# Split values kept in DRAM, the mask built first, affine rows on GpSimd's queue, the attention's merge in halves, and raw tiles of their own for the last output weights

## The chip, the cores and the metric

The kernel runs on one core of a Trainium2 chip. A core has TensorE (PE, with its weight loads PEld), VectorE (DVE), ScalarE (ACT), GpSimd (POOL) and SyncE (SP), which run side by side and wait for each other by semaphores; transfers between DRAM and on-chip memory go through 16 DMA engines, from queues that an engine issues to. The metric is the device time of one execution in microseconds (us); a lower time is better.

## The reference

The kernel computes two layers on 1024 rows of width 1024, in float32. Each layer has a token mixer and then an MLP, each inside `x = LayerNorm(alpha * x + gate * f(x * (1 + scale) + shift))`. Layer 0's mixer is a gated MLP; layer 1's is the attention that the change is about.

```python
def mixer_b(h, w_qkv, w_out, slopes):
    qkv = (h @ w_qkv).reshape(B, S, N_PAT, 3, B_HEADS, B_HEAD_DIM)   # 3 patterns, 16 heads of 64
    for g, (window, dilation) in enumerate(((128, 1), (512, 4), (2048, 16))):
        o, lse = dilated_branch(qkv[:, :, g, 0], qkv[:, :, g, 1], qkv[:, :, g, 2], window, dilation, slopes)
        ...
    wts = softmax(stack(lses, axis=0), axis=0)[..., None]
    o = sum(wts * stack(outs, axis=0), axis=0)
    return o.reshape(B, S, 1024) @ w_out
# dilated_branch: s = q k^T / 8 - slope * dilation * diff, masked to 0 <= diff <= span, softmax, times v
def squared_relu_mlp(h, w_up, w_down):
    return square(relu(h @ w_up)) @ w_down
```

## The kernel before, in words

Every large product is made of three matmuls on float32r operands: each operand is split into a high part (a cast, mostly on ACT, line 102) and a low part (source minus high part, mostly on DVE, line 103), and high x high, high x low and low x high are added up in PSUM. `split` issues the pair. So behind every matmul operand stands one ACT and one DVE operation.

The program runs through the stages in this order: mixer of layer 0, its MLP, `values` (lines 1123 to 1249), `attention` (1252 to 1626), the output projection (`OutRows`), the second MLP. A scheduler orders each engine's instructions by the program's own order and its estimates, except where `tc.keep_in_program_order` pins one; an engine then runs its list strictly in that order. A DMA issue stands in the list of the engine that issues it; here that is always SP. Tiles come from pools in which a tag names a set of buffers; a tile whose tag has n buffers waits until the one n before it is no longer used.

`values` makes the v part of the projection for the three patterns g = 2, 1, 0. Each is a matrix product in seven block products (Strassen's scheme in Winograd's form), in the order 1, 2, 5, 6, 7, 4, 3 (`V_STEPS`), each of four groups (m = 0..3) of twelve matmuls. Product p takes a left form from the activations (`L11`, `L12`, `S1`, `S2`, `S3`, `L22`, `S4`; each in four blocks, high and low) and a right form from the weights (`vrhi`, `vrlo`). The generator `second` builds the forms S1 to S4 and L22 while the first products run; one step of it is taken per group, and a product whose form isn't built takes the steps it still needs. `evict` takes a finished group out of PSUM into `vpart` (ACT copies it, or DVE adds it to an earlier one) and stores finished blocks of v in `v_dram`.

`attention` goes over head pairs hp = 0..7 and patterns g = 2, 1, 0. Each (hp, g) has eight slots, each slot two positions, into which functions are put with `at(slot, position)`; between them the stream of q and k projections runs (`project`, line 1332, psq and psk), which TensorE fills the time with, and which is five chunks of work ahead. In a slot stand scores (`sc`), the exponentials (line 1411), transposes (`pT`), the split of the transposed probabilities (`pThi` on ACT, `pTlo` on DVE) and the product with v (`pv`, line 1459). `near` and `far` are the mask and distance tiles, built on POOL, from which POOL makes a `bias` for each head (line 1393). `qlo` holds the low part of q. `load_v` loads v for a pair, 512 KB, as `v_raw` and splits it into the tile `v`.

Two pieces of work are spread over the slots. `affine_row(i)` applies LayerNorm's gain and bias (`aff_g`, `aff_b`) on POOL to eight rows of tiles that were spilled to DRAM, at slots 2 + 2i; its loads and stores stand on SP. `merge(hp)` puts the three patterns of a pair together: it reads their maxima and sums, makes the three factors, spreads them over partitions by DMA (`bc`), multiplies each pattern's output by its `bc` (line 1543, three operations of 128x1024) and adds them up (line 1546, two operations), at slots base + 5 to base + 7, where base is 8 (3 hp + 3), that is while the next pair's first pattern runs.

At the end the output projection takes eight weight rows `wo_0` to `wo_7` in chunks of two (`unit`: load `wo_raw`, multiply by the gate on POOL, split) and the merged outputs `oraw_k`; weights and outputs from number 4 on share two `raw` buffers. `Residual` loads the rows that are added (`res`, line 289).

## Time and profile before

| | us |
|---|---|
| median of 3 runs (lowest, highest) | 2790.56 (2788.13, 2792.9) |
| the profiled execution's own time | 2792.79 |
| its span | 2791.1 |
| PE busy | 2697.5 (97%) |
| DVE busy | 2036.5 (73%) |
| ACT busy | 1424.1 (51%) |
| POOL busy | 189.2 (7%) |
| mean granted TensorE clock | 0.987 |
| moved by DMA | 416.63 MB, 149 GB/s |

A busy engine is one with an instruction in execution; an instruction that waits is not counted. A row of a timeline gives start, duration, engine, line and operation, its output and inputs by the program's names with buffer numbers left out, and in brackets the idle time of that engine just before it, with what ended it. A row with x2 stands for two instructions that overlap. The profile is of one execution, 2.2 us above the median of the runs.

### The profile page before, as it was taken

To read this page: it belongs to the slowest core of one execution; us is meant where nothing else is said; L and a number is where in the kernel's file an instruction comes from. 1 tells how busy PE (TensorE), PEld (TensorE's weight loads), DVE (VectorE), ACT (ScalarE), POOL (GpSimd) and SP (SyncE) were. 2 spreads that over 40 slices of the span, in tenths; PEclk is the share of its full clock that TensorE was granted. 3 is DMA by queue.
4 is the path that set the end of the run, shared out by engine and by line. 5 is a ranking of instruction groups with operands and counts; after the bars stand their busy time and mean duration, and the time that the engine had idled before them with its cause. 6 is when DMAs were issued, how large, how long until landed. Compare 5 with 4: busy or idle time off the path is not lost.

```text
span 2791.1 us, 36348 instructions
## 1 busy us (share of the span) xinstructions
PE 2697.5 (97%) x12954; PEld 2244.4 (80%) x12954; DVE 2036.5 (73%) x3600; ACT 1424.1 (51%) x2639; POOL 189.2 (7%) x147
## 2 busy tenths in 40 slices
PE   6999999999999999989999999999998999999998
PEld 5787878887888888878888888888876788878887
DVE  6777797777967795445767767767679975668887
ACT  3354375555443553325665666666563755554332
POOL 1001000000000000043111111111020000000000
PEclk9999999999999999999999999999999999999999
DMA  7533347667845545353222213222234564486562
GB/s 257 166 121 107 120 158 226 219 223 273 295 142 191 165 144 158 121 187 101 62 62 78 74 51 85 77 55 78 85 89 154 171 209 154 158 284 210 171 200 90
DMA packets 317690, 416.63 MB, mean 149 GB/s; under 512 B 49164, under 2 KB 174516, under 8 KB 317508
## 3 DMA queue, kind: packets, MB, share of 16 engines
q1 hardware_dynamic: 317508, 414.31, 46.4%
q8 instruction: 101, 1.65, 0.3%
q14 instruction: 81, 0.66, 0.1%
HBM read 317.69 MB, written 96.55 MB: 148 GB/s over the span
## 4 chain that ended last, share of the span: by engine, by line
PE 73%; DVE 14%; DMA 7%; ACT 3%; issue 2%; POOL 1%; SPq 1%; POOLq 0%; DVEq 0%; ACTq 0%
PE psd L949 21%; PE psua L790 8%; PE psq L1332 8%; PE psk L1332 7%; PE psv L1237 7%; PE psuc L790 4%; PE psd_wout L367 3%; DMA adaw<-in_ada_w_dram 3%; PE pv L1459 2%; PE psu L367 2%; PE psd_wo L367 2%; PE psub L790 2%; PE psv L464 1%; DMA bc<-w_dram 1%; PE sc L1404 1%
## 5 line engine op out<-in xcount | busy, mean ns | idle before, releaser
L790 PE MATMUL psua<-right,left 128*128 128x512 f32 x1536 | 366.2, 392 | 3.3 <-ACT right L102 1.7
L949 PE MATMUL psd<-rhi,lhi 128*128 128x512 f32 x896 | 350.5, 391 | 3.0 <-ACT part L821 3.0
L949 PE MATMUL psd<-rlo,lhi 128*128 128x512 f32 x896 | 350.4, 391 | 0.2
L949 PE MATMUL psd<-rhi,llo 128*128 128x512 f32 x896 | 349.8, 390 | 0.0
L790 PEld LDWEIGHTS psua<-right,left 128*128 128x128 f32 x1536 | 288.1, 189 | 65.5 <-DVE right L103 2.9
L1413 ACT ACTIVATE p<-p,stat 128x128 f32<-128x128 f32 (+1 forms) x384 | 171.2, 446 | 147.2 <-DVE stat L1411 142.4
L949 PEld LDWEIGHTS psd<-rhi,lhi 128*128 128x128 f32 x896 | 168.9, 189 | 39.6 <-ACT part L821 3.9
L949 PEld LDWEIGHTS psd<-rlo,lhi 128*128 128x128 f32 x896 | 168.9, 188 | 36.1 <-DVE rlo L103 1.1
L949 PEld LDWEIGHTS psd<-rhi,llo 128*128 128x128 f32 x896 | 169.0, 189 | 35.1
L1332 PE MATMUL psk<-form_L,wk_hi 128*128 128x512 f32 x576 | 186.9, 406 | 9.7 <-DVE qlo L103 9.7
L790 PE MATMUL psuc<-right,left 128*128 128x512 f32 x768 | 187.8, 391 | 0.0
L1332 PE MATMUL psq<-form_L,wq_hi 128*128 128x512 f32 x576 | 184.9, 402 | 0.0
L103 DVE TENSOR_TENSOR pTlo<-pT,pThi 128x512 fp32r<-128x512 f32 (+1 forms) x160 | 99.6, 623 | 108.8 <-ACT pThi L102 108.5
L128 DVE SCALAR_TENSOR_TENSOR adaacc<-adaw,silu_c,adaacc 128x512 f32<-128x512 f32 x168 | 132.4, 799 | 56.0 <-DMA adaw<-in_ada_w_dram 55.1
L790 PEld LDWEIGHTS psuc<-right,left 128*128 128x128 f32 x768 | 143.4, 188 | 30.0 <-DVE right L103 0.5
L103 DVE TENSOR_TENSOR left<-ws,left 128x512 fp32r<-128x512 f32 x128 | 87.9, 688 | 73.0 <-ACT left L102 71.3
L103 DVE TENSOR_TENSOR llo<-lraw,lhi 128x1024 fp32r<-128x1024 f32 x112 | 136.3, 1217 | 0.8 <-ACT lhi L102 0.8
L102 ACT CAST left<-ws 128x512 fp32r<-128x512 f32 x128 | 79.3, 620 | 96.2 <-DVE ws L711 85.5
L1411 DVE CUSTOM_DVE_ANT_0 p<-sc,bias 128x128 f32<-128x128 f32 (+1 forms) x384 | 122.0, 346 | 8.7 <-PE sc L1405 6.2
L102 ACT CAST rhi<-rraw 128x1024 fp32r<-128x1024 f32 x48 | 50.6, 1054 | 142.9 <-issue 113.7
L1332 PEld LDWEIGHTS psk<-form_L,wk_hi 128*128 128x128 f32 x576 | 101.0, 191 | 25.2 <-issue 10.1
L1237 PE MATMUL psv<-vrhi,form_S 128*128 128x512 f32 x384 | 119.4, 389 | 0.2 <-DVE vpart L1214 0.2
(286 smaller groups left out, 6325.8 us busy)
## 6 DMA issues: line engine op xcount, KB each, us to landing
lraw<-forms SPq DMA_DIRECT2D x112, 512.0 KB
adaw<-in_ada_w_dram SPq DMA_DIRECT2D x192, 256.0 KB
up<-in_mlp_w_up_dram SPq DMA_DIRECT2D x64, 512.0 KB
forms<-s SPq DMA_DIRECT2D x128, 256.0 KB
rraw<-in_mlp_w_down_dram SPq DMA_DIRECT2D x64, 512.0 KB
forms<-part SPq DMA_DIRECT2D x96, 256.0 KB
vraw<-in_b_w_qkv_dram SPq DMA_DIRECT2D x26, 512.0 KB
spill<-acc SPq DMA_DIRECT2D x24, 512.0 KB
```

The lines of the kernel that those rows point to most:

```text
L102: first = A.copy(hi, src) if hi_engine is A else hi_engine.tensor_copy(hi, src)
L103: return first, lo_engine.tensor_tensor(lo, src, hi, op=ALU.subtract)
L128: ins = V.scalar_tensor_tensor(acc[:], raw[:], silu_c[:, k : k + 1], acc[:], ALU.mult, ALU.add)
L367: T.matmul(dst, s[a], m[b], start=(n == 0), stop=(n == last))
L464: T.matmul(sums[u, half][:], units[u][a_][:, k * P : (k + 1) * P], hT[half][b_][:, k, :], start=k == 0 and a_ + b_ == 0, stop=k == KD - 1 ...
L790: T.matmul(acc, w[:, a, k, :], right[p][:, b, k, :], start=p in (1, 2, 5) and k + a + b == 0, stop=k == 3 and a == 1, skip_group_check=True)
L949: ins = T.matmul(sums[kind, m][:], l[a][:, k, m * P : (m + 1) * P], r[b][:, k, :], start=p in (1, 5, 2, 3) and kp + k + a + b == 0, stop=k ...
L1237: T.matmul(acc, left[:, a, 2 * kp + k, m * P : (m + 1) * P], r[b][:, k, :], start=p in (1, 2, 5) and kp + k + a + b == 0, stop=kp == 1 and ...
L1332: T.matmul(p[:], wu[a][:, k * P : (k + 1) * P], h_op(k, half, b), start=k + c_ == 0, stop=k == KD - 1 and c_ == 2)
L1411: V.tensor_tensor_reduce(out=pr[:, 0:w], in0=scb[:, sl], in1=st["bias"][:, width - w :], scale=-0.125, scalar=3e38, op0=ALU.add, op1=ALU.m ...
L1413: A.activation(pr[:, 0:w], pr[:, 0:w], AF.Exp, bias=nm, scale=-1.0, accum_out=l)
L1459: T.matmul(pvs[b][:, q0 % HALF : q0 % HALF + w_], stt, x_[:, o_ : o_ + w_], start=not begun[b], stop=left[b] == 0, skip_group_check=True)
```

## The change

Five things are done.

- `evict` no longer stores v as it is: it splits it (ACT and DVE, `vs`, two buffers) and stores both parts, 512 KB a group instead of 256; product 4 is split straight out of PSUM. `load_v` then loads the split tile directly, 1 MB, a position earlier, and has no split. `second` makes a form's `S3` block right after the `S2` block of the same number, in a step of its own, so that one `S3` temporary is enough where four were kept.
- `near`, `far` come before the `qlo` memsets, in another pool.
- The affine rows are loaded and stored by DMAs on POOL's own queue; loads at slots 2 + 3i, the two operations, pinned, at slots 3 + 3i.
- The merge's five operations become ten of half the width, pinned (but for the last pair), one to a position from slot base + 6 to base + 10; the last pair's stand from base + 10 on, two to a position.
- At the end `oraw_4` and `oraw_5` come as one 1 MB load into a v buffer, and `oraw_6`, `wo_6`, `wo_7` have tiles of their own in a pool `late`.

```diff
 def unit(src, name, gate=None, pinned=False, lo_engine=V, to=None, raw=None):
-        raw = wts.tile([P, D], F32, name=f"{name}_raw", tag="raw", bufs=2)
+        if raw is None:
+            raw = wts.tile([P, D], F32, name=f"{name}_raw", tag="raw", bufs=2)[:]
...
@@ values
-            xp = pool(ph, "x_v", 12)
+            xp = pool(ph, "x_v", 9)
+            parted = pool(ph, "parted_v", 2)
...
                 for k in range(4):
-                    s3.append(x_tile(f"s3_{k}"))
-                    sub(s3[k][:], form["L11"][:, 0, k, :], l21[k][:])
-                    plus_lo("L11", k, s3[k][:])
+                    s3 = x_tile(f"s3_{k}")
+                    sub(s3[:], form["L11"][:, 0, k, :], l21[k][:])
+                    plus_lo("L11", k, s3[:])
                     place("L22", k, x22[k][:])
-                    sub(x22[k][:], x22[k][:], s3[k][:])
+                    sub(x22[k][:], x22[k][:], s3[:])
                     place("S2", k, x22[k][:])
                     yield
+                    place("S3", k, s3[:])
+                    yield
                 built.add("S2")
-                for k in range(4):
-                    place("S3", k, s3[k][:])
-                    yield
                 built.update(("S3", "L22"))
...
             def evict(g, p, m):
                 acc = sums["pb" if p in (2, 5, 3) else "pa", m][:]
-                if p in (1, 5, 6, 4):
+                if p in (1, 5, 6):
                     t = parts[p, m] = x_tile(f"vpart_{g}_{p}_{m}")
                     A.copy(t[:], acc)
-                else:
...
+                    return
+                if p != 4:
+                    t = parts.pop(({2: 1, 7: 5, 3: 6}[p], m))
                     V.tensor_tensor(t[:], acc, t[:], op=ALU.add)
+                    acc = t[:]
+                v = parted.tile([P, 4, 4, HEAD], F32R, name=f"vs_{g}_{p}_{m}", tag="vs")
+                split(v[:, :, 0:4:3, :], v[:, :, 1:3, :], acc.rearrange("p (h e c) -> p h e c", e=2, c=HEAD))
...
+                nc.sync.dma_start(v_dram[g][i * P : (i + 1) * P, 4 * dh : 4 * dh + 4, :],
+                                  v[:].rearrange("p h f c -> p h (f c)").bitcast(F32))
@@ attention
-                @at(max(base - 4, 0), 1)
+                @at(max(base - 4, 0), 0)
                 def load_v():
...
-                    my["v"] = vs = qp.tile([P, NT, 4, HEAD], F32R, name=f"v_{hp}_{g}", tag="v")
-                    split(vs[:, :, 0:4:3, :], vs[:, :, 1:3, :], raw[:].rearrange("p t (e c) -> p t e c", e=2))
@@ merge
-                    V.tensor_tensor(bc, o, bc, op=ALU.mult)
+                    n = o.shape[1] // 2
+                    o, bc = (t[:, half * n : (half + 1) * n] for t in (o, bc))
+                    in_order(V.tensor_tensor(bc, o, bc, op=ALU.mult))
...
+                for n, f in enumerate(steps):
+                    n = n + 12 if hp < N_PAIRS - 1 else n // 2 + 10
+                    at(base + n // 2, n % 2)(f)
@@ affine rows
+                affine["row"] = row_bc(f"aff_{i}")
+                nc.gpsimd.dma_start(affine["row"][:], spill[1][i * P : (i + 1) * P, :])
+
+            def affine_row(i):
+                t = affine["row"]
+                for n, op in (("g", ALU.mult), ("b", ALU.add)):
+                    tc.keep_in_program_order(G.tensor_tensor(t[:], t[:], affine[n][:], op=op))
+                nc.gpsimd.dma_start(spill[1][i * P : (i + 1) * P, :], t[:])
 
             for i in range(NT):
-                at(2 + 2 * i, 1)(lambda i=i: affine_row(i))
+                at(2 + 3 * i, 0)(lambda i=i: affine_load(i))
+                at(3 + 3 * i, 1)(lambda i=i: affine_row(i))
@@ the output weights
+                    both = qp.tile([P, 2, S], F32, name="oraw_4", tag="v")
+                    nc.sync.dma_start(both[:], o_dram[4:6].rearrange("k p t -> p k t"))
...
+        late = pool(ph, "late", 1)
+        for n in ("w6", "w7", "o6"):
+            out.raws[n] = late.tile([P, D], F32, name=f"late_{n}")[:]
```

What this does to the order on POOL where the attention begins (a row: line, operation, output<-inputs with buffer numbers, shape); before:

```order
L1577 TENSOR_TENSOR aff_1_10499<-aff_1_10499,aff_g_10412 128x1024
L1578 TENSOR_TENSOR aff_1_10499<-aff_1_10499,aff_b_10414 128x1024
L1577 TENSOR_TENSOR aff_2_10585<-aff_2_10585,aff_g_10412 128x1024
L1578 TENSOR_TENSOR aff_2_10585<-aff_2_10585,aff_b_10414 128x1024
L1577 TENSOR_TENSOR aff_3_10663<-aff_3_10663,aff_g_10412 128x1024
L1578 TENSOR_TENSOR aff_3_10663<-aff_3_10663,aff_b_10414 128x1024
L1271 IOTA near_10127 128x256
L1272 AFFINE_SELECT near_10127<-near_10127 128x256
L1274 AFFINE_SELECT near_10127<-near_10127 128x256
```

and after:

```order
L1596 TENSOR_TENSOR aff_0_10513<-aff_0_10513,aff_g_10509 128x1024
L1596 TENSOR_TENSOR aff_0_10513<-aff_0_10513,aff_b_10511 128x1024
L1597 DMA spill_1_105<-aff_0_10513 128x1024
L1273 IOTA near_10243 128x256
L1284 MEMSET qlo0_0_10254 64x1024
L1274 AFFINE_SELECT near_10243<-near_10243 128x256
L1284 MEMSET qlo1_0_10256 64x1024
L1276 AFFINE_SELECT near_10243<-near_10243 128x256
L1591 DMA aff_1_10634<-spill_1_105 128x1024
L1596 TENSOR_TENSOR aff_1_10634<-aff_1_10634,aff_g_10509 128x1024
L1596 TENSOR_TENSOR aff_1_10634<-aff_1_10634,aff_b_10511 128x1024
```

The iota and the two selects that make `near` stood behind rows `aff_1`, `aff_2`, `aff_3`; now they stand behind `aff_0` alone, and the DMAs of the rows stand among POOL's own instructions.

On DVE in `values`, from the third block of `S2` (`form_S2`) on, before:

```order
L103 TENSOR_TENSOR form_S2_8539<-l22_2_8619,form_S2_8539 128x512
L1157 TENSOR_TENSOR l22_3_8652<-l22_3_8652,s3_3_8764 128x512
L103 TENSOR_TENSOR vrlo_2_6_1_8774<-v_t_1_8473,vrhi_2_6_1_8773 128x1024
L103 TENSOR_TENSOR form_S2_8539<-l22_3_8652,form_S2_8539 128x512
L103 TENSOR_TENSOR form_S3_8540<-s3_0_8687,form_S3_8540 128x512
L103 TENSOR_TENSOR form_S3_8540<-s3_1_8711,form_S3_8540 128x512
L1101 TENSOR_TENSOR vraw_2_7_0_8747<-v_r22_0_8474,vraw_2_7_0_8747 128x1024
```

and after:

```order
L103 TENSOR_TENSOR form_S2_8542<-l22_2_8625,form_S2_8542 128x512
L1161 TENSOR_TENSOR s3_3_8822<-form_L11_8098,l21_3_8484 128x512
L1164 TENSOR_TENSOR l22_0_8551<-l22_0_8551,form_L12_8099 128x512
L1164 TENSOR_TENSOR s3_3_8822<-s3_3_8822,form_L11_8098 128x512
L1104 TENSOR_TENSOR vraw_2_7_0_8756<-v_r22_0_8477,vraw_2_7_0_8756 128x1024
L1161 TENSOR_TENSOR l22_3_8661<-l22_3_8661,s3_3_8822 128x512
L103 TENSOR_TENSOR form_S3_8543<-s3_3_8822,form_S3_8543 128x512
L103 TENSOR_TENSOR form_S4_8544<-l22_0_8551,form_S4_8544 128x512
L103 TENSOR_TENSOR form_S2_8542<-l22_3_8661,form_S2_8542 128x512
L103 TENSOR_TENSOR vrlo_2_7_0_8838<-vraw_2_7_0_8756,vrhi_2_7_0_8837 128x1024
```

The fourth block of `S2`, which came three instructions of DVE behind the third one's, now comes eight behind it; two blocks of `S4`'s work, a right form for product 7 (`vraw_2_7`) and the last `S3` block stand between. Counted from the first `vpart_2_1_0` of product 2, the fourth block was 30 instructions behind; now it is 42.

On DVE at the merge of pair 2, around the split `pTlo_7_2_0` (`bc_2_0`, `bc_2_1`, `bc_2_2` are the merge's tiles), before:

```order
L103 TENSOR_TENSOR k1_3_1_13564<-psk_3_1_0_13665,k1_3_1_13564 64x4x128
L1543 TENSOR_TENSOR bc_2_0_13629<-oT_2_0_13358,bc_2_0_13629 128x1024
L1411 ISA p_7_2_5_13744,stat_3_2_13446<-sc_7_2_2_13736,bias_7_2_13652 128x128
L1411 ISA stat_3_2_13446 128x1
L1546 TENSOR_TENSOR bc_2_0_13629<-bc_2_0_13629,bc_2_1_13623 128x1024
L103 TENSOR_TENSOR pTlo_7_2_0_13769<-pT_7_2_0_13763,pThi_7_2_0_13768 128x512
L1546 TENSOR_TENSOR bc_2_0_13629<-bc_2_0_13629,bc_2_2_13626 128x1024
```

and after:

```order
L103 TENSOR_TENSOR k1_3_1_13668<-psk_3_1_0_13772,k1_3_1_13668 64x4x128
L1556 TENSOR_TENSOR bc_2_1_13727<-oT_2_1_13125,bc_2_1_13727 128x512
L1418 ISA p_7_2_5_13843,stat_3_2_13550<-sc_7_2_2_13835,bias_7_2_13756 128x128
L1418 ISA stat_3_2_13550 128x1
L103 TENSOR_TENSOR pTlo_7_2_0_13868<-pT_7_2_0_13862,pThi_7_2_0_13867 128x512
L1556 TENSOR_TENSOR bc_2_2_13730<-oT_2_2_12781,bc_2_2_13730 128x512
L1418 ISA p_7_2_6_13883,stat_3_2_13550<-sc_7_2_3_13878,bias_7_2_13756 128x128
L1418 ISA stat_3_2_13550 128x1
L1418 ISA p_7_2_7_13886,stat_3_2_13550<-sc_7_2_3_13878,bias_7_2_13756 128x128
L1418 ISA stat_3_2_13550 128x1
L1556 TENSOR_TENSOR bc_2_2_13730<-oT_2_2_12781,bc_2_2_13730 128x512
```

Before, a whole product and a whole sum stood just ahead of `pTlo_7_2_0`; now one half product does, and the next half follows it.

## What I expect

> **What bounds the kernel now.** I read the totals first, then the busy time stage by stage, then the list of what TensorE waited for, and last the instructions around each wait. From the page's head and from the table of stretches (span of the stretch, PE, PEld, DVE, ACT and POOL busy time, granted TensorE clock, DMA share, GB/s):
>
> ```profile
> span 2791.1 us, 36348 instructions
> PE 2697.5 (97%) x12954; PEld 2244.4 (80%) x12954; DVE 2036.5 (73%) x3600; ACT 1424.1 (51%) x2639; POOL 189.2 (7%) x147
> 994.00:1050.00 56.00, 55.76 (x262) 46.15 (x262) 52.22 (x81) 35.25 (x52) 0.00 (x0) 1.00 0.49 165
> 1050.00:1227.00 177.00, 177.00 (x783) 146.56 (x782) 86.11 (x87) 57.01 (x74) 12.56 (x7) 1.00 0.44 142
> 1227.00:1300.00 73.00, 63.30 (x306) 52.90 (x305) 33.67 (x71) 30.70 (x66) 38.06 (x23) 0.93 0.52 165
> 1300.00:2000.00 700.00, 682.09 (x3860) 586.84 (x3859) 490.03 (x1239) 439.37 (x1125) 79.85 (x83) 0.99 0.26 68
> 2000.00:2120.00 120.00, 109.68 (x533) 89.46 (x533) 90.66 (x179) 60.33 (x144) 24.52 (x13) 0.93 0.39 120
> ```
>
> TensorE is busy for 2697.5 of 2791.1 us, so all its idle time together is 93.6 us, and nothing that the change does to the other engines counts unless it shortens or lengthens a TensorE wait or moves its clock. The change touches four stages: values (994 to 1227), the start of attention (1227 to 1300), its body (to about 2000) and its tail. TensorE is idle there for 0.2, 9.7, 17.9 and 10.3 us. In the first 56 us of values VectorE is busy for 52.2, which matters below. The waits of TensorE from 990 to 2210 (engine, line, what it waited for, us in total, times, longest):
>
> ```profile
> PE pv L1459 <- DVE pTlo L103: 17.3, 7, 2.5
> PE psk L1332 <- DVE qlo L103: 9.7, 1, 9.7
> PE psd_wo L367 <- DVE wo_lo L103: 2.4, 1, 2.4
> PE psd_wo L367 <- ACT wo_hi L102: 2.1, 1, 2.1
> ```
>
> So the prizes are one wait of 9.7 us, seven waits of about 2.5 us, and two in the last output matmuls. Around the first, from the timelines of POOL, DVE and PE, with the clock of those 20 us:
>
> ```profile
> 1205.36 2.39 POOL L1578 TENSOR_TENSOR aff<-aff,aff_b 128x1024 f32<-128x1024 f32 x1
> 1241.35 2.35 POOL L1578 TENSOR_TENSOR aff<-aff,aff_b 128x1024 f32<-128x1024 f32 x1
> 1244.97 0.23 DVE L1277 COPY far<-near 128x128 f32<-128x128 f32 x1 [10.30 <-POOL near L1274]
> 1245.11 0.68 DVE L103 TENSOR_TENSOR qlo<-psq,q 64x512 fp32r<-64x512 f32 x1
> 1236.20 0.61 PE L1332 MATMUL psq<-form_L,wq_hi 128*128 128x512 f32 x2
> 1236.88 0.61 PE L1332 MATMUL psq<-form_L,wq_hi 128*128 128x512 f32 x2
> 1248.10 1.19 PE L1332 MATMUL psk<-form_L,wk_hi 128*128 128x512 f32 x2 [9.70 <-DVE qlo L103]
> 1253.36 0.66 PE L1332 MATMUL psk<-form_L,wk_hi 128*128 128x512 f32 x2
> 1240.00:1260.00 20.00, 11.90 (x42) 9.62 (x43) 8.06 (x11) 6.04 (x8) 14.06 (x11) 0.74 0.57 172
> ```
>
> The mask's `far` copy stands ahead of the `qlo` split on VectorE, it waits 10.30 us for `near`, and `near` stands on POOL behind four affine rows that wait for their loads, the last of them done at 1243.7. When TensorE resumes at 1248.10 it is slow: twelve matmuls take 5.26 us up to 1253.36, where three take 0.68 us before (1236.20 to 1236.88), so 2.5 us more are lost to the clock. That stall costs 12.2 us.
>
> Around one of the seven, the merge of head pair 2, and what the clock does in two stretches with a merge:
>
> ```profile
> 1588.77 2.03 DVE L1543 TENSOR_TENSOR bc<-oT,bc 128x1024 f32<-128x1024 f32 x1 [1.02 <-DMA bc<-w_dram]
> 1596.97 1.22 DVE L1546 TENSOR_TENSOR bc<-bc,bc 128x1024 f32<-128x1024 f32 x1
> 1598.11 0.68 DVE L103 TENSOR_TENSOR pTlo<-pT,pThi 128x512 fp32r<-128x512 f32 x1
> 1598.85 0.33 PE L1459 MATMUL pv<-pTlo,v 128*128 128x128 f32 x1 [2.50 <-DVE pTlo L103]
> 1480.00:1520.00 40.00, 37.08 (x194) 31.45 (x193) 29.25 (x65) 22.03 (x58) 4.30 (x4) 0.91 0.35 94
> 1580.00:1620.00 40.00, 37.50 (x217) 32.20 (x216) 31.54 (x77) 23.18 (x64) 4.71 (x5) 1.00 0.41 107
> ```
>
> Five whole merge operations (2.03 us where the input is strided, 1.22 where not) come within 11 us on a VectorE that has its usual work as well, and `pTlo` is late by 2.50 us. The clock is 0.91 in one stretch (0.09 x 40 = 3.6 us) and 1.00 in the other, so a merge costs between 2.5 us and about 6; over the 682 busy us of the attention's body a mean clock of 0.99 is some 7 us.
>
> **The cost of each part.**
>
> *Mask first.* On POOL the mask now stands behind one affine row instead of four, so it is ready before the first `qlo` needs it. In the trace that one row is done at 1207.75, and TensorE asks for `qlo` at 1238.4, 9.70 us ahead of 1248.10; the `qlo` split itself takes 0.68, so nothing else on VectorE holds it. The gain is the whole stall at most, 9.7 if the clock still dips for another reason, and 0 if POOL starts 30 us later. I take 12.
>
> *Merge in halves.* Ten half operations per merge, one per half slot, in pinned order. A half costs about 1.02 us strided (half of 2.03) and at most 0.69 else, and `pTlo` waits behind one half instead of a whole one of 1.22 and its neighbours. Laid against the times of this merge, `pTlo` of the four places comes 0 to 0.4 us after TensorE wants it. I leave 0.8 us for each of seven merges and no dip: 17.3 and 7 less 5.6 is a gain of 18. The ends are 24 (no wait left) and 8 (two waits of 1.2 us per merge, no cooling). The exponentials queued behind a half wait for its `bc` load too, as they do now.
>
> *v kept split in DRAM.* The attention drops these two groups, and values takes them over:
>
> ```profile
> L103 DVE TENSOR_TENSOR v<-v_raw,v 128x1024 fp32r<-128x1024 f32 x24 | 29.3, 1222 | 2.2 <-ACT v L102 2.1
> L102 ACT CAST v<-v_raw 128x1024 fp32r<-128x1024 f32 x24 | 25.2, 1048 | 12.1 <-DMA v_raw<-v 11.5
> ```
>
> Those 54.5 us lie beside matmuls; apart from easing the merges they are worth 0 on the path, and the DMA bytes it adds (12.6 MB each way) have room at the 0.44 and 0.26 shares of the table. The cost is in values: 48 more VectorE subtractions of 128x512 (0.69 each, 33 us) and 48 casts on ACT less 12 copies. From 1050 on VectorE has 91 us free and hides them. In the first 56 us it has 3.8 us free. There the order of the work counts:
>
> ```profile
> 1012.51 0.69 DVE L1214 TENSOR_TENSOR vpart<-psv,vpart 128x512 f32<-128x512 f32 x1
> 1013.11 0.68 DVE L103 TENSOR_TENSOR form_L<-l,form_L 128x512 fp32r<-128x512 f32 x1
> 1028.68 1.22 DVE L1098 TENSOR_TENSOR v_t<-v_r,v_t 128x1024 f32<-128x1024 f32 x1
> 1029.82 0.69 DVE L103 TENSOR_TENSOR form_S<-l,form_S 128x512 fp32r<-128x512 f32 x1
> 1032.17 0.69 DVE L103 TENSOR_TENSOR form_S<-l,form_S 128x512 fp32r<-128x512 f32 x1
> 1020.47 0.50 PE L1237 MATMUL psv<-vrhi,form_S 128*128 128x512 f32 x1 [0.24 <-DVE vpart L1214]
> ```
>
> Back to back, VectorE starts a 128x512 operation every 0.60 us (1012.51, 1013.11) and a 128x1024 one every 1.14 (1028.68, 1029.82). Product 5 starts at 1020.47, and four groups of twelve matmuls at 0.227 take 10.9 us, so product 6, which needs `S2`, starts at 1031.4 and needs the fourth block of `S2`, low part included, at 1034.1. Before, that is the operation at 1032.17. In the changed order it stands 42 operations behind the one at 1012.51: four splits of `vs` are new, the `S3` blocks are placed between the `S2` blocks, and `S4` and product 7 have moved ahead of it. That is 38 x 0.60 + 4 x 1.14 = 27.4 us, so it starts at 1039.9 and ends at 1040.6. TensorE loses 6.5 us there, in waits of 1 to 4 us, and 1.5 us of clock; VectorE, which the later products leave idle, is caught up by product 7. I take a loss of 8. The ends are 0 (the total of VectorE's work is only 5.5 us more than fits, some of it is ready earlier than I think) and 11 (6.5, the 2.5 of clock seen at the mask, and 2 for a `vs` buffer that waits for its store; there are two).
>
> *Affine rows on POOL's own queue.* The sixteen operations of 2.4 us are the same; a row now has three of the attention's 192 slots, which lie between 1227 and about 2040, so 4.2 us each and 12.6 a row. Most rows now fall into the attention. In the stretch from 1227 to 1300 POOL is busy for 38 us, most of it affine rows, and apart from the 9.7 TensorE is not idle: beside such rows the attention keeps up. The trace has no DMA issued by POOL; the nearest rows are SP's, the slowest of them in the tail below (six in 11.83 us, 2.0 each with their waits). Two per row make 4 us of POOL's time, in a row's 12.6 of which the two operations take 4.8: it fits, so the one end is 0, and the other, if each of eight rows makes `pTlo` late by 0.6, is 5. A gain has no reason on the path beyond the mask's. I take a loss of 1, near the stretch's row. Behind POOL's waits stand the bias rows and the second halves of `q`, which the scores of a slot need.
>
> *The tail.* Two output weights come late:
>
> ```profile
> 2086.06 2.04 DVE L1543 TENSOR_TENSOR bc<-oT,bc 128x1024 f32<-128x1024 f32 x1 [6.68 <-DMA bc<-w_dram]
> 2124.51 0.69 DVE L387 TENSOR_TENSOR acc<-acc,psd_wo 128x512 f32<-128x512 f32 x1 [2.19 <-PE psd_wo L367]
> 2098.69 11.83 SPq L289 DMA_DIRECT2D res<-spill  x6
> 2115.56 0.50 PE L367 MATMUL psd_wo<-wo_lo,oTs 128*128 128x512 f32 x1 [2.45 <-DVE wo_lo L103]
> 2117.52 0.63 PE L367 MATMUL psd_wo<-wo_hi,oTs 128*128 128x512 f32 x1
> 2127.26 0.63 PE L367 MATMUL psd_wo<-wo_hi,oTs 128*128 128x512 f32 x2
> ```
>
> TensorE waits 2.45 and 2.12 us for weights 6 and 7, whose raw tiles come free late and whose loads stand behind six residual loads on SP (11.83 us), and from about 2117.5 to 2127.3 a single matmul takes 0.63 us, as long as a pair at 2127.26: about half the rate. Less the wait of 2.12 that is 7.7 us of work, so 3.8 lost. With tiles of their own, loaded early, all 8.4 could go. But VectorE is then the bound: from the merge of the last pair at 2086.06 on it has some 30 us of work without a gap (that merge's halves, the sums of the finished chunks, six residuals, the last four `oTs` and two weight splits) ahead of the first sum of the last chunk, which comes at about 2117 instead of 2124.51. I take 6.5; the ends are 8.4 and 0 (the merge of the last pair, or the gate multiply on POOL, takes the weights' place).
>
> *Sum.* -12 - 18 + 8 + 1 - 6.5 = -27.5. The profiled execution took 2792.79 us (its span and 1.7 around it), which makes 2765.3; it stands 2.2 above the median of the runs shown, 2790.56, and against that the same difference makes 2763, which I forecast.
>
> **The Trainium skill on the clock.** The table of the clock's states in "TensorE: Matmul & The Clock Gate" (Part 1) says that the clock falls to half after an idle window of about 3.4 us. Here it had fallen at 2117.52, after one wait of 2.45 us, so the trace does not hold to that figure. By the page, none of the waits at merges and tail would cool the clock and the 10.8 us of clock in the sum would stay: 2774.
>
> "DMA: Bandwidth & Descriptors" (SWDGE vs HWDGE vs iDMA) says that GpSimd writes its descriptors into SBUF, where VectorE can lock it out. No run here shows it. It would lengthen the waits of the slower rival below.
>
> **Rivals.** (a) *Values keep up* after all: the operations ahead of `S2` are hidden, so 8 less, 2755. For it: 0.2 us of waits there before. Against it: 52.2 of 56 us busy already, and the order. (b) *Merges keep half their waits*: the halves are spread, but VectorE is 70% busy in this stage (490 of 700) and more around a merge, and `pTlo` meets a half, a weight split and an exponential in a row: gain 8 instead of 18, 2773. (c) *The mask is not earlier*, because POOL's first loads now stand ahead of it and wait for their memory: 12 more, 2775. Against it: POOL's first row has 30 us to spare, as above. (d) *Slower:* POOL is held by its own DMAs. One buffer carries all affine rows, so each load waits for the store of the row before, and the `q` copies and biases behind it wait as well. If such a wait is of the size of the 10.30 us that `far` waited, less the 6 us by which the store goes ahead, each of eight rows costs 4 us and 1.5 of clock: 44 us, 2807. It decides from 3.5 us lost per row. Against it: a row's store is issued one and a half slots (6 us) ahead of the next load. (e) *The clock dips as often as before*, whatever becomes of the waits: 7 and 3.8 stay, 2774. Against it: 1.00 in the stretch from 1580. The clock page named above gives the same time.
>
> **Chances.** My forecast 2763, for itself 2757 to 2769: 0.48. (a) 0.18, (b) 0.15, (c) 0.04, (e) 0.03, (d) 0.06; several small losses together that leave it within 0.2% (5.6 us, about what a measurement of this kernel can tell from no change): 0.06. The range 2750 to 2782 holds (a) with its own spread, (b), (c) and (e), and leaves out (d) and the last. Faster 0.88, same 0.06, slower 0.06.
>
> **What would show it.** Right: no wait of `psk` for `qlo` and a clock near 1.00 from 1240 on; waits of `psv` for `form_S` or its split near 1033 to 1041, 5 to 8 us of TensorE idle time in values; waits of `pv` for `pTlo` below 6 us in all, with whole stretches at 1.00; `psd_wo` without the 2.45 and 2.12. Wrong: no wait in values at all (then 2755); `sc` or `pT` waiting for POOL's `bias` or `q` in the first eight slots of rows (then (d)); `pv` still waiting for over 10 us. My weakest step is the 6.5 us in values, which rests on VectorE staying saturated and in that order.

## The result, and the profile after

The changed kernel takes 2775.20 us (median of five runs, 2769.43 to 2780.09), against 2792.9 (2788.13 to 2795.81) for the kernel before on the same chip: a ratio of 0.9937 with a 95% interval of 0.9917 to 0.9957. It is faster by 17.7 us, where 27.5 were forecast; that lies within the range, but above the 2757 to 2769 that the forecast gave itself. The profiled execution took 2770.57 us; its span is 22.3 us shorter than that of the profiled one of before, 4.6 more than the medians' difference.

From the page of the changed kernel, the head and TensorE's totals, and from the table of stretches the same ones as before (PE, PEld, DVE, ACT and POOL busy time, granted clock, DMA share, GB/s):

```profile
span 2768.8 us, 36382 instructions
PE 2682.1 (97%) x12954; PEld 2227.8 (80%) x12954; DVE 2042.6 (74%) x3664; ACT 1420.4 (51%) x2651; POOL 192.9 (7%) x165
```

```profile
994.00:1050.00 56.00, 54.65 (x254) 43.86 (x253) 51.72 (x79) 35.95 (x55) 0.00 (x0) 1.00 0.46 160
1050.00:1227.00 177.00, 177.00 (x783) 146.56 (x782) 112.16 (x129) 71.51 (x101) 18.24 (x15) 1.00 0.59 205
1227.00:1300.00 73.00, 66.83 (x325) 55.93 (x324) 37.47 (x79) 32.89 (x76) 18.17 (x16) 0.95 0.48 145
1300.00:2000.00 700.00, 685.89 (x3917) 587.44 (x3916) 475.94 (x1266) 424.69 (x1114) 101.58 (x102) 1.00 0.34 91
2000.00:2120.00 120.00, 109.15 (x533) 89.34 (x533) 98.29 (x213) 58.88 (x132) 20.76 (x11) 0.96 0.48 148
```

From 1227 to 2000 there is more of TensorE's work in each stretch, and the clock is at least as high in all of them; values has lost a little (1.35 us idle, before 0.24). The last stretch holds more of the tail than it did, so its busy times don't compare. What TensorE waits for from 990 to 2210 has changed its names:

```profile
PE pT L1446 <- ACT p L1420: 11.3, 17, 1.5
PE psk L1340 <- DVE qlo L103: 6.2, 1, 6.2
PE pv L1466 <- DVE pTlo L103: 5.3, 7, 1.2
PE psd_wo L368 <- DVE acc L388: 3.0, 3, 1.3
PE psd_wo L368 <- DVE wo_lo L103: 1.8, 1, 1.8
PE psv L1244 <- DVE vpart L1218: 0.9, 2, 0.6
```

The waits of `pv` for `pTlo` fell from 17.3 to 5.3 us, but waits of `pT` for the exponentials `p` are new, 11.3. The one wait of `psk` for `qlo` is still there, 6.2 instead of 9.7. There is no wait for `form_S` in values.

The 22.3 us between the two profiled executions, by when TensorE reaches the same instruction, fall as follows:

| piece | change, us | forecast |
|---|---|---|
| before values (not touched by the change) | -2.2 | 0 |
| values, to the first `psq` (1227.36, now 1227.19) | +2.1 | +8 |
| attention's start, to the first `psk` (1248.10, now 1244.40) | -3.5 | -12 (mask) |
| to the first merge | -0.6 | +1 (affine) |
| first to seventh merge (605.8, now 595.9) | -9.9 | -18 |
| seventh merge to the last `pstat` | +1.1 | 0 |
| last `pstat` to the first waiting transpose `pst` of the projection's result (72.1, now 63.7) | -8.4 | -6.5 |
| the rest | -0.9 | 0 |

The merges' gain came out at about half, the mask's at less than a third, the loss in values at a quarter, and the tail did as forecast. The first row shows how much one execution can say: the stretch before values is the same in all fourteen kernels profiled here, and it takes between 989.0 and 1000.0 us. The experiments follow these pieces.

### The profile page after: what moved, and what is told of

Same layout as the page of the kernel before. It is cut to its first block, busy times and chain, and to the rows that moved or that the text cites. A ratio compares the mean times of both kernels' runs of the same rounds, so it can differ in the third digit from the quotient of the medians.

```text
span 2768.8 us, 36382 instructions
## 1 busy us (share of the span) xinstructions
PE 2682.1 (97%) x12954; PEld 2227.8 (80%) x12954; DVE 2042.6 (74%) x3664; ACT 1420.4 (51%) x2651; POOL 192.9 (7%) x165
## 4 chain that ended last, share of the span: by engine, by line
PE 67%; DVE 17%; DMA 7%; ACT 5%; issue 3%; POOL 0%; SPq 0%; DVEq 0%; ACTq 0%; POOLq 0%
PE psd L951 22%; PE psk L1340 7%; PE psua L792 7%; PE psq L1340 6%; PE psv L1244 6%; DMA adaw<-in_ada_w_dram 3%; PE psuc L792 3%; PE psd_wout L368 3%; PE psu L368 2%; PE pv L1466 2%; PE psv L466 2%; DVE adaacc L128 1%; PE psub L792 1%; DVE left L103 1%; PE psd_wo L368 1%
## 5 line engine op out<-in xcount | busy, mean ns | idle before, releaser
L102 ACT CAST lhi<-lraw 128x1024 fp32r<-128x1024 f32 x112 | 117.3, 1047 | 3.2 <-PE psua L792 2.9
```

The lines of the kernel that those rows point to most:

```text
L102: first = A.copy(hi, src) if hi_engine is A else hi_engine.tensor_copy(hi, src)
```

## The experiments

Each was timed against the kernel before on its own chip, whose median lay between 2790.94 and 2792.90 us there; the ratio is to that.

| kernel | median us (lowest to highest) | ratio (95%) |
|---|---|---|
| the changed kernel | 2775.20 (2769.43 to 2780.09) | 0.9937 (0.9917 to 0.9957) |
| pe_pinned | 2778.91 (2778.19 to 2782.65) | 0.9959 (0.9947 to 0.9971) |
| no_store | 2765.61 (2760.52 to 2774.78) | 0.9913 (0.9898 to 0.9927) |
| v_only | 2788.55 (2778.52 to 2794.47) | 0.9988 (0.9973 to 1.0004) |
| v_whole | 2761.06 (2758.83 to 2763.66) | 0.9893 (0.9880 to 0.9906) |
| mask_only | 2790.52 (2784.66 to 2801.42) | 1.0000 (0.9987 to 1.0012) |
| aff_sp | 2769.61 (2764.80 to 2773.66) | 0.9930 (0.9917 to 0.9942) |
| vw_mask_late | 2767.15 (2761.61 to 2768.92) | 0.9912 (0.9890 to 0.9933) |
| vw_aff_sp | 2766.90 (2765.90 to 2768.83) | 0.9914 (0.9896 to 0.9932) |
| merge_whole | 2787.11 (2773.85 to 2794.89) | 0.9976 (0.9960 to 0.9992) |
| merge_earlier | 2764.58 (2763.33 to 2770.57) | 0.9910 (0.9895 to 0.9924) |
| vw_earlier | 2763.92 (2760.34 to 2770.75) | 0.9910 (0.9887 to 0.9932) |
| tail_old | 2782.14 (2778.66 to 2785.68) | 0.9970 (0.9959 to 0.9981) |

### Why values kept up: TensorE's own order (pe_pinned)

The fourth block of `S2` was late on VectorE as forecast: its split is the second of the pair at 1037.70 of the changed kernel's timeline. The forecast had it start at 1039.9, which is 1037.7 here, where values start 2.2 us earlier. The product that needs it did not stop:

```profile
1037.70 1.28 DVE L103 TENSOR_TENSOR form_S<-l,form_S 128x512 fp32r<-128x512 f32 x2
1018.77 0.50 PE L1244 MATMUL psv<-vrhi,form_S 128*128 128x512 f32 x1 [0.59 <-DVE vpart L1218]
```

TensorE's largest wait from 1017 to 1042 is this 0.59 us. The order on TensorE shows why. In the changed kernel, the matmuls of product 6 for the last group (`psv1_2_3`) are followed by ones that were left over of the first group (`psv1_2_0`):

```order
L1244 MATMUL psv1_2_3_8564<-vrhi_2_6_0_8729,form_S2_8542 128x512
L1244 MATMUL psv1_2_3_8564<-vrhi_2_6_1_8776,form_S2_8542 128x512
L1244 MATMUL psv1_2_3_8564<-vrlo_2_6_1_8777,form_S2_8542 128x512
L1244 MATMUL psv1_2_0_8489<-vrhi_2_6_1_8776,form_S2_8542 128x512
L1244 MATMUL psv1_2_0_8489<-vrlo_2_6_1_8777,form_S2_8542 128x512
```

Before, each group was finished ahead of the next. The scheduler now does the blocks that are ready for all four groups first, and the late one last. The prediction looked at VectorE's order alone. The experiment pins TensorE's order, group by group, in these steps; VectorE's order stays what it is in the changed kernel.

```diff
-    T.matmul(acc, left[:, a, 2 * kp + k, m * P : (m + 1) * P], ...)
+    ins = T.matmul(acc, left[:, a, 2 * kp + k, m * P : (m + 1) * P], ...)
+    if n in (3, 4):
+        tc.keep_in_program_order(ins)
```

> The changed kernel, with the matmuls of products 6 and 7 of the first pattern pinned to the order group by group; VectorE's order stays as it is in the changed kernel, where the fourth block of S2 ended at 1038.4. Theory A (in the changed kernel TensorE did not wait for S2 only because its matmuls were issued in another order, the ready blocks of all groups first): product 6 starts near 1029.7 and needs that block at 1032.4, so TensorE waits about 6 us for form_S between 1030 and 1039, with 1.5 of clock behind it: 2782 to 2783 against the changed kernel's 2775.2. Rival B (S2 is ready in time anyway, the place is not tight): waits in values stay below 2 us, 2775.

TensorE's timeline of pe_pinned:

```profile
1035.09 0.50 PE L1244 MATMUL psv<-vrhi,form_S 128*128 128x512 f32 x1 [0.63 <-ACT form_S L102]
1036.25 0.50 PE L1244 MATMUL psv<-vrhi,form_S 128*128 128x512 f32 x1 [0.42 <-DVE form_S L103]
1040.79 0.79 PE L1244 MATMUL psv<-vrhi,form_S 128*128 128x512 f32 x1 [4.03 <-ACT form_S L102]
```

and its first stretch of values:

```profile
994.00:1050.00 56.00, 50.30 (x223) 40.07 (x222) 51.71 (x82) 35.45 (x54) 0.00 (x0) 0.94 0.44 156
```

The waits of 5.1 us appear at the forecast place, with a clock of 0.94 in the stretch (0.06 x 56 = 3.4 us). From their start to the first `psq`, values take 241.6 us here, 234.7 in the changed kernel and 232.6 in the kernel before: a loss of 9.0 where 8 was forecast. So the stall of 8 was a right reading of VectorE and a wrong one of TensorE. By the median the old order costs 3.7 us, less than the 6.9 of the traces; the intervals of the two kernels overlap, so the trace, not the time, carries this.

### What took the mask's place at attention's start (no_store, v_only)

The mask was ready at 1211.7, long before use. The first `psk` still waited. From the changed kernel's timelines of PE, ACT and DVE:

```profile
1244.40 1.19 PE L1340 MATMUL psk<-form_L,wk_hi 128*128 128x512 f32 x2 [6.17 <-DVE qlo L103]
1231.96 0.62 ACT L102 CAST vs<-vpart 128x512 fp32r<-128x512 f32 x1 [5.00 <-DMA v<-vs]
1234.64 2.63 DVE L103 TENSOR_TENSOR vs<-vpart,vs 128x512 fp32r<-128x512 f32 x1 [0.73 <-ACT vs L102]
1237.79 2.79 DVE L103 TENSOR_TENSOR wq_lo<-wq_raw,wq_hi 128x1024 fp32r<-128x1024 f32 x1
1241.64 0.68 DVE L103 TENSOR_TENSOR vs<-vpart,vs 128x512 fp32r<-128x512 f32 x1
1242.24 0.67 DVE L103 TENSOR_TENSOR qlo<-psq,q 64x512 fp32r<-64x512 f32 x1
```

and from its chain of work (start, us, what):

```profile
1225.69 6.17 DMA v<-vs
```

The last `vs` splits of values stand ahead of `qlo` on both engines. There are two `vs` buffers; one comes free when its store of 512 KB has landed, which took 6.17 us here. The cast waits 5.00 us for that, and `qlo` stands behind. The prediction had this wait only as an end of the range in values, where TensorE has other work; here, at the last groups, the attention's first casts stand right behind. The experiment leaves out the stores of pattern 0's v; attention loads pattern 1's instead, as many bytes.

```diff
-                nc.sync.dma_start(v_dram[g][i * P : (i + 1) * P, ...
+                if g > 0:
+                    nc.sync.dma_start(v_dram[g][i * P : (i + 1) * P, ...
...
-                    src = v_dram[g][:, hp, :]
+                    src = v_dram[max(g, 1)][:, hp, :]
```

> The changed kernel without the stores of pattern 0's split v (the attention reads pattern 1's in their place, so its output is not the reference's). Theory A (the 6.2 us wait of psk for qlo at the attention's start comes from the two vs buffers waiting for their stores to land: ACT waited 2.9, 4.1 and 5.0 us for v<-vs there, and the splits stand ahead of qlo on VectorE): those waits of ACT go, the wait of psk falls to 1.5 or less, and 1.3 of clock with it: 2768 to 2770, from 2775.2. Rival B (the splits themselves, slowed on VectorE by POOL's affine rows to 2.6 to 3.4 us, make qlo late): the wait stays at 4 us or more, 2773 to 2776.

The `psk` wait is gone altogether, and TensorE has no idle time from 1240 to 1260. The changed kernel:

```profile
1240.00:1260.00 20.00, 15.60 (x58) 12.77 (x59) 8.72 (x11) 5.60 (x8) 3.74 (x6) 0.83 0.95 263
```

and no_store:

```profile
1240.00:1260.00 20.00, 20.00 (x94) 16.67 (x94) 8.38 (x14) 8.19 (x12) 3.21 (x5) 1.00 0.71 195
```

The wait of 6.2 and 0.17 x 20 = 3.4 us of clock make 9.6. From the first `psq` to the first `pstat` no_store takes 126.5 us where the changed kernel takes 135.3, 8.8 less; the median is 9.6 lower (the intervals just overlap). The wait for the store is the cause: the two slow operations of the changed kernel's rows, 2.63 and 2.79 us, have their like in no_store, also ahead of `qlo`, and there TensorE does not wait (that without the stores the DMA engines are less busy as well, 0.71 against 0.95, was not separated):

```profile
1232.19 2.82 DVE L103 TENSOR_TENSOR wk_lo<-wk_raw,wk_hi 128x1024 fp32r<-128x1024 f32 x1
1234.94 2.88 DVE L103 TENSOR_TENSOR vs<-vpart,vs 128x512 fp32r<-128x512 f32 x1
```

The kernel before with the v split alone:

```diff
 # the kernel before, with evict, second, v_dram and load_v of the changed kernel
```

> The kernel before with v kept split in DRAM, and nothing else changed. Theory A (the split is a loss by itself: values take 1.5 to 2 us more, the wait of psk at the attention's start stays at 6 to 10 us, and the whole merges' seven waits stay at 16 us or more): 2792 to 2797 against before's 2791 to 2793. Rival B (the 54 us that leave VectorE and ACT in the attention are a gain, and only its meeting with the other parts turned it into a loss): 2787 or less, with waits for pTlo of 12 us or less.

2788.55 us, no measurable difference (the interval reaches 1.0004), with a `psk` wait of 3.2 and the merges' waits for `pTlo` unchanged at 17.2. The wait expected at the start was too large: alone, the split even shortens it from 9.7. Its timelines show why: the mask's `far` copy, which stood ahead of `qlo` on VectorE, comes behind it here (1244.64, `qlo` at 1242.59), and what holds `qlo` is again a `vs` cast that waits 5.26 us for a store. From the first `psq` to the first `psk` v_only takes 6.5 us less than the kernel before, and 4.3 more from the first `pstat` to the seventh.

### v whole, and the other half of the mask's gain (v_whole, mask_only, vw_mask_late, vw_aff_sp, aff_sp)

If the stores hold the start, the rest of the change should do better without the split in values:

```diff
 # the changed kernel, with evict, second, v_dram and load_v of the kernel before
-    v_dram = [dram.tile([S, N_PAIRS, 4 * HEAD], F32, name=f"v_{g}") for g in range(3)]
+    v_dram = [dram.tile([S, D], F32, name=f"v_{g}") for g in range(3)]
```

> The changed kernel with v stored whole and split in the attention, as before; mask, merge, affine rows and tail stay changed. Theory A (the split store brings the new wait at the attention's start, since vs has two buffers that wait for 512 KB stores, and gives the path little in return): the 6.2 us wait of psk for qlo goes, with 1.3 of clock, values take 1.4 us less, and the merges get 2 to 4 us of waits back: 2769 to 2772. Rival B (taking the 54 us of splits out of the attention is what makes the halves fit): waits of pv for pTlo go from 5 to 12 us or more, and the time is 2780 or more.

2761.06 us, 14.1 below the changed kernel and 31.6 below the kernel before; it beats both. It is lower than even the theory that blamed the split had said, because the merges improved too (next part). From its list of waits:

```profile
PE pT L1443 <- ACT p L1417: 6.2, 14, 1.4
PE pv L1463 <- DVE pTlo L103: 2.7, 5, 1.0
PE psk L1336 <- DVE qlo L103: 1.4, 2, 1.0
```

Here the mask's gain is whole: the `psk` waits fell from 9.7 to 1.4. Is it the mask alone? The next two are the mask in the kernel before, and the mask late in v_whole:

```diff
 # mask_only: the kernel before, with
+            near = ql.tile([P, 2 * P], F32, name="near")
+            ... iota, the two selects, far
             qlo = [[ql.tile([P, S], F32R, name=f"qlo{e}_{b}") ...
-            near = qp.tile([P, 2 * P], F32, name="near", bufs=1)
-            ... iota, the two selects, far
 # vw_mask_late: v_whole, with this block as it was before
```

> The kernel before with the mask first, and nothing else changed. Theory A (the whole stall at the attention's start was the mask's; in the changed kernel the store waits took its place): the wait of psk for qlo goes from 9.7 to below 1.5 us, the clock there stays at 1.00, and the time is 11 to 12 us below before: 2781 against 2792.9. Rival B (another input of the qlo split is late by itself, so that the mask was worth only the 3.5 us seen in the changed kernel): the wait stays at 5 us or more, 2788 to 2790.

> As v_whole (v stored whole, the other four parts changed; 2761.1, psk waited 1.4 us for qlo), but with the mask where it was before, behind affine row 2 on POOL. Theory A (mask and queue each take away one of two waits that end within a few us of each other, so either alone gives little): far waits for near until about 1241, psk waits 4 to 9 us for qlo, with 1 to 2.5 of clock: 2766 to 2772. Rival B (with the rows off SP the mask is early enough anyway): the wait stays below 2.5 us, 2761 to 2763.

mask_only gains nothing (ratio 1.0000); its `psk` waits 8.5 us. vw_mask_late waits 7.2 and takes 2767.15. What still holds mask_only is a v cast on ACT. ACT and SP of mask_only:

```profile
1247.36 1.04 ACT L102 CAST v<-v_raw 128x1024 fp32r<-128x1024 f32 x1 [9.79 <-DMA v_raw<-v]
1236.93 0.34 SPq L1578 DMA_DIRECT2D spill<-aff  x1
1240.48 0.69 SPq L1378 DMA_DIRECT2D v_raw<-v  x1
```

and of v_whole:

```profile
1236.59 1.05 ACT L102 CAST v<-v_raw 128x1024 fp32r<-128x1024 f32 x1 [2.06 <-DMA v_raw<-v]
1229.48 0.69 SPq L1383 DMA_DIRECT2D v_raw<-v  x1
```

In mask_only the load of `v_raw` stands on SP behind an affine row's store, which waits for POOL, and the load of the next row; it is issued at 1240.48, in v_whole at 1229.48. ACT waits 9.79 us for it, with the cast of q behind. So the affine queue, which I had priced as a loss of 1, would be the second half of the mask's gain. The test puts the rows back on SP, at the slots of before and not pinned, with v whole and with v split:

```diff
-                nc.gpsimd.dma_start(affine["row"][:], spill[1][i * P : (i + 1) * P, :])
+                nc.sync.dma_start(t[:], rows)
...
-                at(2 + 3 * i, 0)(lambda i=i: affine_load(i))
-                at(3 + 3 * i, 1)(lambda i=i: affine_row(i))
+                at(2 + 2 * i, 1)(lambda i=i: affine_row(i))
```

> As v_whole, but with the affine rows loaded and stored from SP, as before. Theory A (their stores wait for POOL at the head of SP's list and hold back v_raw, whose cast and split stand ahead of the second half's qlo): psk waits 7 to 9 us for qlo, as with the mask alone, with 1.5 to 2.5 of clock: 2769 to 2773. Rival B (the queue is worth nothing, as I predicted with a loss of 1): the wait stays below 2.5 us, 2760 to 2763.

> The changed kernel with the affine rows loaded and stored from SP at slots 2 + 2i and not pinned, as before. Theory A (the queue is worth nothing on the path, a loss of 1 us at most as predicted): 2773 to 2777, waits in the first 150 us of attention within 2 us of the changed kernel's. Rival B (on SP a row's store, which waits for POOL, stands ahead of vs stores, projection weights and v loads): the wait of psk for qlo grows to 9 us or more, or sc waits for q, and the time is 2780 or more.

With v whole: `psk` waits 7.9 and 2766.90 us; this and vw_mask_late are 6 us above v_whole by the medians, with intervals that overlap its own a little. The kernels with v whole then stand so at the `psk` wait: neither part 9.7 (the kernel before), mask alone 8.5 and 7.9 (mask_only, vw_aff_sp), queue alone 7.2, both 1.4. Neither part is worth much without the other, since each ends a wait that hides the other's. (What is called the queue here is the queue with the slots and the pinning that came with it; they were not taken apart.)

With v split, neither theory had it: `psk` waits 2.9 where the changed kernel has 6.2, and the time is not told apart (the intervals overlap). There is no v cast to hold, so SP's order does no harm; and POOL's row, which in the changed kernel runs beside the two slow operations above, stands elsewhere:

```profile
1234.31 2.41 POOL L1596 TENSOR_TENSOR aff<-aff,aff_g 128x1024 f32<-128x1024 f32 x1 [5.76 <-DMA aff<-spill]
1236.80 2.70 POOL L1596 TENSOR_TENSOR aff<-aff,aff_b 128x1024 f32<-128x1024 f32 x1
```

In the changed kernel VectorE's two operations at 1234.64 and 1237.79 last 2.63 and 2.79 us instead of 0.69 and 1.22: 3.5 us, about the difference of the two waits (3.2). In aff_sp the rows are at 1223.64 and 1244.36, and no such operation comes ahead of `qlo`; a `vs` cast waits 5.54 us for its store there. The traces together separate the two: slow operations without the store's wait cost nothing (no_store), the store's wait without slow operations costs 2.9 (aff_sp) or 3.2 (v_only), both together 6.2. No run moves the row's place and nothing else.

### Where the merges' gain went (merge_whole, merge_earlier, vw_earlier)

```diff
 # merge_whole: whole products and sums as before, not pinned
-                    at(base + n // 2, n % 2)(f)
+                    at(base + 5 + n // 2, n % 2)(f)
```

> The changed kernel with the merge in five whole operations, not pinned, at the slots of before. Theory A (the halves are what shortened the seven waits): waits of pv for pTlo return to 15 to 17 us from 5.3, the seven waits of 1.3 us of pT for p go (8.8 us), the clock dips to 0.92 behind some merges (4 us): 2775 + 11 - 9 + 4 = 2781, between 2779 and 2785. Rival B (VectorE was relieved by the splits that left the attention, so that whole merges no longer hurt): waits below 8 us in all, 2770 or less.

2787.11 by the median, with a wide spread (2773.85 to 2794.89): some 12 us above the changed kernel, and 17.1 us of `pTlo` waits as before. The run undoes the halves, the pinning and the slots together. So the merge in halves does what it was meant to. (The profiled execution of merge_whole, 2776.97 us, is one of its fast ones and does not show where all of the 12 us go.) But in the changed kernel a new wait comes with the merges. DVE, ACT and PE in the merge of pair 2:

```profile
1603.43 0.29 DVE L1418 CUSTOM_DVE_ANT_0 p<-sc,bias 128x128 f32<-128x128 f32 x1
1603.76 0.69 DVE L103 TENSOR_TENSOR qlo<-psq,q 64x512 fp32r<-64x512 f32 x1
1604.47 0.69 DVE L1560 TENSOR_TENSOR bc<-bc,bc 128x512 f32<-128x512 f32 x1
1605.19 0.42 DVE L1418 CUSTOM_DVE_ANT_0 p<-sc,bias 128x256 f32<-128x256 f32 x1
1605.66 0.51 ACT L1420 ACTIVATE p<-p,stat 128x256 f32<-128x256 f32 x1 [0.89 <-DVE stat L1418]
1606.32 0.33 PE L1446 MATMUL pT<-ident,p 128*128 128x128 f32 x1 [1.26 <-ACT p L1420]
```

The last half sum (1604.47) and a `qlo` split (1603.76) stand between the two exponentials of a slot, in the next pattern's slots, those of pattern 1, where some of the tiles are longer (128x256). The second exponential comes late, ACT after it, and TensorE's transpose waits 1.26 us. At the first six merges such a wait takes 1.25 to 1.52 us, 7.8 of the 11.3; at the seventh it is 0.53. In v_whole the same half stands behind both, and so does the `qlo` split:

```profile
1594.12 0.29 DVE L1415 CUSTOM_DVE_ANT_0 p<-sc,bias 128x128 f32<-128x128 f32 x1
1594.34 0.42 DVE L1415 CUSTOM_DVE_ANT_0 p<-sc,bias 128x256 f32<-128x256 f32 x1
1595.51 0.69 DVE L1557 TENSOR_TENSOR bc<-bc,bc 128x512 f32<-128x512 f32 x1
```

Nothing of the merge differs between the two kernels; in the attention only `load_v`, with its casts and splits, is another, and the scheduler placed what is around it in another order. The test moves the halves one slot earlier, out of that place, in both:

```diff
-                    n = n + 12 if hp < N_PAIRS - 1 else n // 2 + 10
+                    n = n + 10 if hp < N_PAIRS - 1 else n // 2 + 10
```

> The changed kernel with the ten half operations of a merge one slot earlier, so that the last one no longer stands on VectorE between the exponentials of the second pattern's third slot. Theory A (the seven waits of 1.3 us of pT for p come from that last half ahead of an exponential): they go, 8.8 us less, 2766 to 2768; waits for pTlo stay at 4 to 6 us. Rival B (bc has not landed a slot earlier, or another place is as tight): the wait moves, pv for pTlo or sc grows by as much, 2773 to 2777.

> As v_whole, with the merge's halves one slot earlier. Theory A (in v_whole the last half already stands behind the exponentials, so there is nothing to gain, and two halves now stand ahead of pTlo): 2761 to 2766, waits for pTlo 3 to 8 us against 2.7. Rival B (a slot earlier is better in itself, as it was in the changed kernel by 10 us): 2752 to 2757, waits of pT for p of 3 us or less against 9.1.

merge_earlier takes 2764.58 us, 10.6 less than the changed kernel by the medians (the intervals overlap a little, 0.9917 to 0.9924), and TensorE's waits are:

```profile
PE psk L1340 <- DVE qlo L103: 5.4, 1, 5.4
PE pv L1466 <- DVE pTlo L103: 5.4, 7, 1.2
PE pT L1446 <- ACT p L1420: 3.6, 7, 0.8
PE pT L1443 <- ACT p L1420: 2.0, 1, 2.0
```

The wait at the exponentials is gone at the first merge and 0.54 to 0.79 us at the next five, where the `qlo` split still stands between them. In the profiled executions, which are 7.2 us apart, the move saves 4.8 between the first and the seventh merge and 2.0 from there to the last `pstat`; the wait for `qlo` at the attention's start stays. In vw_earlier, where the place was not bad, the move gains nothing: 2763.92, with 10.4 us of `pTlo` waits where v_whole has 2.7. So the place of the last half cost the changed kernel here; that it is worse only with v split is a product of the scheduler's order.

### The tail (tail_old)

```diff
-        late = pool(ph, "late", 1)
-        for n in ("w6", "w7", "o6"):
-            out.raws[n] = late.tile([P, D], F32, name=f"late_{n}")[:]
 # and oraw_4 to oraw_7 singly, in the two "raw" buffers, as before
```

> The changed kernel with the last weights and outputs in the two shared raw buffers, as before. Theory A (their late loads cost the 8 us that the tail gained): psd_wo waits again for wo_lo and wo_hi, 2 to 2.5 us each, with half the clock behind them: 2782 to 2784. Rival B (VectorE is the bound of the tail anyway, and the smaller halves of the merge gave the gain): 2775 to 2778.

2782.14, 6.9 above the changed kernel, the intervals apart. TensorE at the largest waits of the projection, in tail_old:

```profile
2094.08 0.50 PE L368 MATMUL psd_wo<-wo_hi,oTs 128*128 128x512 f32 x1 [3.22 <-DVE acc L388]
2111.19 0.50 PE L368 MATMUL psd_wo<-wo_lo,oTs 128*128 128x512 f32 x1 [3.04 <-DVE wo_lo L103]
```

and in the changed kernel:

```profile
2080.20 0.50 PE L368 MATMUL psd_wo<-wo_hi,oTs 128*128 128x512 f32 x1 [1.32 <-DVE acc L388]
2099.92 0.50 PE L368 MATMUL psd_wo<-wo_lo,oTs 128*128 128x512 f32 x1 [1.84 <-DVE wo_lo L103]
```

From the last `pstat` to the last `psd_wo` tail_old takes 84.6 us, the kernel before 84.4 and the changed kernel 76.1. With tiles of their own the weights are no longer what is waited for most in all; small waits for VectorE's sums (`acc`) are, 3.0 us together, though the longest single wait, 1.84, is still for a weight. VectorE is busy for 49.3 of the 50 us from 2080 on, where it was for 39.8 before.

## Why the prediction was right or wrong

The sign was right and the time is inside the range, but that is in part luck: the sum was the result of errors that partly cancel. Of the four signs of being right, two came (waits of `pv` below 6 us, `psd_wo` without its two long waits) and two did not (`psk` still waited for `qlo`, and no wait for `form_S` came).

- **Values, +8; measured +2.1, of which 1.1 is more TensorE idle time (1.35 against 0.24).** The failed step is "product 6, which needs `S2`, starts at 1031.4 and needs the fourth block": it took TensorE's order as unchanged. VectorE's timing held, and with TensorE's old order the forecast waits came (pe_pinned). What rival (a) said came about, no wait for `S2`, but not for its reason: VectorE's operations were not hidden, TensorE took other work first. It weighs more that the split cost elsewhere: v_whole is 14.1 faster. The step "apart from easing the merges they are worth 0 on the path" failed at the attention's start, where the `vs` splits and their stores now hold `qlo`; whether the merges are eased turned on the halves' slot (below).
- **Mask, -12; measured -3.5.** The mask was early, as said. The failed step is that "nothing else on VectorE holds" `qlo`: the `vs` splits did, held by their own stores (no_store), and with v whole a v load on SP would have (vw_aff_sp). A stall has a second late arrival behind it, and I did not look for it.
- **Merges, -18; measured -9.9 between the first and the seventh.** The mechanism was right: `pTlo` waits of 5.3 where 5.6 were forecast, and a clock of 1.00 in that stretch, so rival (e) fell. What was mis-sized is the rest: the term had no wait for the halves at the end of the row, the last of which now stands ahead of an exponential: 7.8 us of waits, of which moving it a slot took away 4.8 (merge_earlier).
- **Affine rows, +1.** With v whole they are worth 5.8 (vw_aff_sp against v_whole); with v split no difference is told. The failed step is "a gain has no reason on the path beyond the mask's". Rival (d) fell: in the list of TensorE's waits none is for POOL's `bias` or `q`.
- **Tail, -6.5; measured -8.4 in the profile, and 6.9 by tail_old.** Right; VectorE's sums are what is waited for next, as forecast.

Where the split's cost lies is read from the profiled executions, by when TensorE reaches the same instruction. The left column is the changed kernel less v_whole, the right one the same with the halves a slot earlier, merge_earlier less vw_earlier:

| piece, us more with v split | halves as in the change | a slot earlier |
|---|---|---|
| before values (the same in all) | -3.3 | +1.7 |
| values | +2.2 | +2.8 |
| first `psq` to first `psk` | +5.7 | +4.6 |
| to the first `pstat` | +1.0 | +0.8 |
| first to seventh `pstat` | +9.6 | -5.5 |
| to the last `pstat` | -3.6 | +0.5 |
| the rest | +0.1 | -3.1 |
| together | 11.7 | 1.8 |

From values to the first `pstat` the split costs 8 to 9 us in both. Between the merges it loses with the halves in one slot and gains in the other, where the splits that left the attention ease VectorE (`pTlo` waits of 5.4 against 10.4). So the 14.1 is not the price of the split by itself: merge_earlier and vw_earlier are 0.7 us apart by the medians and are not told apart. v_only, with whole merges, is a third case. What stays open: about 1 us of the loss in values, and the 1.1 between the seventh merge and the last `pstat`, beyond the clock's fall below.

## What to carry to other kernels

When a wait is removed, list everything that stands ahead of the waiting instruction on its engine and ask when each would be ready; the gain ends at the second latest, and a short ring of buffers whose stores must land is a candidate at the end of a stage, where no other work covers it. Where a scheduler orders the engines, compare the order of the consumer as well as that of the producer, and time a part in company: mask and queue took 1.2 to 2.5 us off one wait alone and 8.3 together, and the split cost 14.1 us with the merge in one slot and nothing measurable with it one slot earlier. A piece put between two operations of a chain costs as a wait even if its engine is 70% busy.

## What the hardware showed that was not expected

The clock also falls without a long wait. In the changed kernel, after 2015, in stretches of 5 us:

```profile
2015.00:2020.00 5.00, 2.71 (x12) 1.98 (x13) 4.91 (x5) 4.09 (x9) 1.15 (x1) 0.75 0.29 100
2020.00:2025.00 5.00, 3.20 (x11) 2.31 (x12) 3.73 (x12) 2.55 (x7) 4.14 (x2) 0.50 0.41 123
```

No wait there is over 1.41 us, but TensorE is busy for only 5.9 of 10 us, and the clock is 0.50 in the second 5. The single waits of 1.26 us at the merges left it at 1.00. Nor does the length of one wait decide: behind the `psk` wait of 3.25 us in v_only the next pair of matmuls took 0.70 us, at full clock, and behind that of 2.95 us in aff_sp 1.19 us, at a falling one. The Trainium skill, in "TensorE: Matmul & The Clock Gate" (Part 1), gives an idle window of about 3.4 us for that fall; read as one idle time, this trace does not agree, since none there is as long.

POOL's own DMAs for the affine rows cost POOL 0.53 to 0.61 us each to issue, also while VectorE is busy:

```profile
1239.92 0.61 POOL L1597 DMA_DIRECT2D spill<-aff  x1 [0.42 <-POOL aff L1596]
```

The Trainium skill states in "DMA: Bandwidth & Descriptors" (SWDGE vs HWDGE vs iDMA) that VectorE, in one of its modes, locks GpSimd out of the memory that holds its descriptors. No run here shows such a lock-out.

And VectorE's operations beside an affine row on POOL can last far longer, 2.63 and 2.79 us where 0.69 and 1.22 are usual, as shown at the attention's start; the prediction had counted POOL's rows as harmless there. Not every operation there is slow: `vpart` at 1237.19, which reads PSUM (`psv`), took its usual 0.68 us beside the same row.
